# Transposes of q, k and the softmax moved from TensorE to VectorE and DMA, one group's values in one go, the narrow gates in another place

## The chip, the cores and the metric

The kernel runs on one core of a Trainium2 chip. The metric is device time in microseconds (us) of one execution of the whole program; less is better. The engines are named as the profile names them: PE (TensorE: matmuls, and PEld its weight loads), DVE (VectorE), ACT (ScalarE), POOL (GpSimd) and SP (SyncE, which here only issues DMAs).

## What is computed

Two layers of a decoder on 512 tokens of width 1024, all in float32. Each layer has a recurrent branch and an attention branch from one wide projection, gates that merge the two, an output projection, and a gated MLP. The attention has 12 heads of 128 in three groups with dilations 1, 4 and 16, whose results are merged by their softmax sums.

```python
def reference(x, positions, ln1_g, w_in, ...):
    for l in range(DEPTH):
        h = rms_norm(x, ln1_g[l])
        z = h @ w_in[l]                      # 1024 -> 8704 columns
        xr, gr, q, k, v, g_rnn, g_att = jnp.split(z, cuts, axis=-1)
        xr = causal_depthwise_conv(xr, rnn_conv_w[l], rnn_conv_b[l])
        hr = rg_lru(xr, lru_wa[l], ...)       # h_t = a_t h_(t-1) + u_t, both from gates of 128x128 blocks
        y_rnn = hr * jax.nn.gelu(gr)
        y_att = dilated_attention_mixer(q, k, v, positions, q_norm_g[l], k_norm_g[l])
        merged = jax.nn.sigmoid(g_rnn) * (y_rnn @ proj_rnn[l]) + jax.nn.sigmoid(g_att) * (y_att @ proj_attn[l])
        x = x + merged @ w_out[l]
        h2 = rms_norm(x, ln2_g[l])
        u = causal_depthwise_conv(h2 @ w_up[l], ffn_conv_w[l], ffn_conv_b[l])
        u_gate, u_val = jnp.split(u, 2, axis=-1)
        x = x + (jax.nn.gelu(u_gate) * u_val) @ w_down[l]
```

Ahead of the scores, q and k are normalised and rotated per head; the probabilities of a group are weighted by its share of the merged softmax and multiplied with the values.

## The kernel before

**Matmuls.** A float32 product is made of three matmuls on operands split into a high and a low part (`mm3`, L257 to L260: high by high, low by high, high by low). The weights come in 320 units of 512 KB from DRAM into one of two buffers (`wraw<-wst`, issued by SP); ACT casts the unit to its high part (`whi`, L228), DVE subtracts to get the low part (`wlo`, L233), each into one of three buffers. A unit is used by 24 matmuls of 512 columns. The cast of a unit may start when PE has left the unit three before it, so it runs two units ahead of its use.

**Groups.** `layer_groups` lists the groups of 512 output columns of a layer in the order in which PE takes them: N1 P1 v0 va P2 N2 P3 P4 vb (q, k and v of the attention; N for the dilation of 1, P for the two others), then xr0 gr0 xr1 gr1 (recurrence and its GeLU gate), ga0 pa0 ga1 pa1 (gate and projection of the attention), gn0 pr0 gn1 pr1 (gate and projection of the recurrence), wo0 wo1 and the MLP.

**Chains.** What follows a group on ACT and DVE, and the small matmuls of scores, values and recurrent gates, is written as generators (chains) that yield `need(engine, time, ...)`. While the main loop records the large matmuls, a planner with a model of each engine's time records steps of these chains between them, as soon as the model holds their operands for ready and a buffer is free (21 slots of 128x512, 12 quads of 128x2048 and a few PSUM banks). A group that needs the result of chains (pa0, pa1, pr0, pr1) forces the rest of them to be recorded first. The order on each engine is thus fixed when the program is built; at run time the engines only wait for each other's results.

**Transposes.** In `QK.block` (L633) each 128x512 piece of q and k (four heads, or four streams of them) is turned by four PE matmuls against an identity (`transpose`, L263, seen as L264) into a PSUM bank; ACT and DVE split it from there. In `attention` (L751), for each of the four passes of a layer, `values_perm` (L813) and `values_nat` (L844) turn the weighted probabilities in the same way, two banks each; `values_nat`, for the dilation of 1, does turn, split and matmuls for one half and then for the other. Each layer so has 156 such matmuls, 312 in all.

**The recurrence.** `lru_weights` (L876) loads and splits the 128x128 gate blocks; it waits for the chain of the fourth attention pass. `XR` (L899) then makes gates, scan and result, one chain for each half (xr0, xr1), each with three quads and more; `GR` (L963) multiplies the GeLU gate's columns by the scan's result and splits the product into the operands of pr0 and pr1, with two quads, after the XR chain of its half.

## Time and profile before

| | before |
|---|---|
| time, median of 3 runs | 1874.34 us (1870.73 to 1874.37) |
| the profiled execution's own time | 1873.33 us |
| its span, first to last instruction | 1871.5 us |
| PE busy | 1862.1 us, 99% of the span |
| DVE busy | 1243.6 us, 66% |
| ACT busy | 951.6 us, 51% |
| granted TensorE clock, mean | 0.999 of full speed |
| DMA | 194 MB, mean 104 GB/s; queue of the weights 28.3% of 16 engines |

PE's busy time is that of the modelled ends of its matmuls, and neighbours overlap; what one matmul costs is read from the distance between two starts. The page's line for an engine counts busy time and instructions; "idle before" in a group is the engine's idle time just ahead of its instructions, with what ended it.

### The profile page before, as it was taken

The numbers are of one execution on the slowest core, as the hardware profiler recorded it, in microseconds if no ns is written. First come the engines' busy times: TensorE is split into PE (matmuls) and PEld (weight loads), VectorE is DVE, ScalarE is ACT, GpSimd is POOL, SyncE is SP. The second block draws the span as 40 slices with busy tenths as digits, with TensorE's granted clock in tenths as the row PEclk, the third lists the DMA queues.
The fourth block names the chain that finished last, engine by engine and source line by source line (L and its number), as shares of the span: only waits on it lengthen the run. The fifth ranks groups of instructions, "written<-read, shape, count | busy, mean of one in ns | idle before, by whom it ended". The sixth has DMA issues, their size and how long they took to land.

```text
span 1871.5 us, 22327 instructions
## 1 busy us (share of the span) xinstructions
PE 1862.1 (99%) x8561; PEld 1547.1 (83%) x8561; DVE 1243.6 (66%) x1858; ACT 951.6 (51%) x1655; POOL 5.6 (0%) x12
## 2 busy tenths in 40 slices
PE   9999999999999999999999999999999999999999
PEld 7888888888888888888888888888888888888887
DVE  7859976884466763577377599778644677536662
ACT  7758855952344342344365687568423444323441
POOL 0000000000000000000000000000000000000000
PEclk9999999999999999999999999999999999999999
DMA  5232233222322222222332322322223222222222
GB/s 177 96 126 95 85 114 113 79 98 96 144 90 102 90 103 100 90 96 96 127 125 86 130 95 102 104 101 79 102 98 138 91 101 91 101 102 90 102 102 90
DMA packets 68106, 194.07 MB, mean 104 GB/s; under 512 B 17312, under 2 KB 17568, under 8 KB 67488
## 3 DMA queue, kind: packets, MB, share of 16 engines
q1 hardware_dynamic: 61824, 183.97, 28.3%
q0 software_dynamic: 1664, 8.39, 1.3%
q8 instruction: 67, 1.10, 0.2%
q10 hardware_dynamic: 4512, 0.30, 0.2%
q14 instruction: 39, 0.32, 0.1%
HBM read 184.19 MB, written 8.44 MB: 103 GB/s over the span
## 4 chain that ended last, share of the span: by engine, by line
PE 97%; DVE 1%; DMA 1%; ACT 1%; issue 0%; ACTq 0%; DVEq 0%
PE acc L258 31%; PE acc L260 31%; PE acc L259 31%; PE at L264 2%; DVE slot L233 1%; PE at L259 1%; PE at L258 1%; PE at L260 1%; PE y L833 1%; PE at L739 0%; DMA stp<-stats 0%; DMA stats<-st 0%; DMA wraw<-wst 0%; PE y L834 0%; PE y L259 0%; PE y L260 0%
## 5 line engine op out<-in xcount | busy, mean ns | idle before, releaser
L228 ACT CAST whi<-wraw 128x1024 fp32r<-128x1024 f32 (+1 forms) x321 | 334.7, 1043 | 596.4 <-PE acc L259 512.5
L233 DVE TENSOR_TENSOR wlo<-wraw,whi 128x1024 fp32r<-128x1024 f32 (+1 forms) x321 | 390.4, 1216 | 253.4 <-ACT whi L228 253.2
L258 PE MATMUL acc<-xh,whi 128*128 128x512 f32 x1280 | 501.1, 391 | 0.0
L260 PE MATMUL acc<-xh,wlo 128*128 128x512 f32 x1280 | 498.4, 389 | 0.0
L259 PE MATMUL acc<-xl,whi 128*128 128x512 f32 x1280 | 498.2, 389 | 0.0
L260 PEld LDWEIGHTS acc<-xh,wlo 128*128 128x128 f32 x1280 | 240.3, 188 | 50.5
L259 PEld LDWEIGHTS acc<-xl,whi 128*128 128x128 f32 x1280 | 240.5, 188 | 48.7
L258 PEld LDWEIGHTS acc<-xh,whi 128*128 128x128 f32 x1280 | 240.4, 188 | 48.6
L258 PE MATMUL acc<-quad,whi 128*128 128x512 f32 x640 | 249.0, 389 | 0.0
L259 PE MATMUL acc<-quad,whi 128*128 128x512 f32 x640 | 249.0, 389 | 0.0
L260 PE MATMUL acc<-quad,wlo 128*128 128x512 f32 x640 | 249.0, 389 | 0.0
L258 PE MATMUL acc<-whi,xh 128*128 128x512 f32 x576 | 231.4, 402 | 1.7 <-ACT whi L228 1.7
L259 PE MATMUL acc<-wlo,xh 128*128 128x512 f32 x576 | 225.5, 391 | 0.2 <-DVE wlo L233 0.2
L260 PE MATMUL acc<-whi,xl 128*128 128x512 f32 x576 | 225.5, 392 | 0.0
L233 DVE TENSOR_TENSOR slot<-acc,rbc 128x512 f32<-128x512 f32 x120 | 82.7, 689 | 129.4 <-PE acc L260 129.4
L258 PEld LDWEIGHTS acc<-quad,whi 128*128 128x128 f32 x640 | 120.2, 188 | 24.9
L259 PEld LDWEIGHTS acc<-quad,whi 128*128 128x128 f32 x640 | 120.2, 188 | 24.9
L260 PEld LDWEIGHTS acc<-quad,wlo 128*128 128x128 f32 x640 | 120.2, 188 | 24.9
L260 PEld LDWEIGHTS acc<-whi,xl 128*128 128x128 f32 x576 | 108.4, 188 | 23.7
L258 PEld LDWEIGHTS acc<-whi,xh 128*128 128x128 f32 x576 | 108.6, 189 | 22.3 <-ACT whi L228 2.2
L259 PEld LDWEIGHTS acc<-wlo,xh 128*128 128x128 f32 x576 | 108.8, 189 | 21.1 <-DVE wlo L233 1.1
L228 ACT CAST quad<-quad 128x512 fp32r<-128x512 f32 x80 | 49.8, 623 | 82.3 <-DVE quad L233 82.2
(142 smaller groups left out, 1928.2 us busy)
## 6 DMA issues: line engine op xcount, KB each, us to landing
wraw<-wst SPq DMA_DIRECT2D x319, 512.0 KB, 3.2
quad<-xT SPq DMA_DIRECT2D x16, 256.0 KB, 5.4
vorder<-quad POOLq DMA_DIRECT2D x4, 1024.0 KB, 5.6
quad<-vorder POOLq DMA_DIRECT2D x4, 1024.0 KB, 5.8
slot<-gqk SPq DMA_DIRECT2D x12, 256.0 KB, 3.5
slot<-lruw SPq DMA_DIRECT2D x8, 256.0 KB, 5.1
xdram<-quad SPq DMA_DIRECT2D x8, 256.0 KB, 2.9
quad<-xdram SPq DMA_DIRECT2D x8, 256.0 KB, 5.3
```

The costliest lines, as they stand in the source:

```text
L228: nc.scalar.copy(out, src)
L233: nc.vector.tensor_tensor(out, a, b, op=op)
L258: nc.tensor.matmul(ps, rr(ah), rr(bh), start=first, stop=False)
L259: nc.tensor.matmul(ps, rr(ah), rr(bl), start=False, stop=False)
L260: nc.tensor.matmul(ps, rr(al), rr(bh), start=False, stop=last)
L264: nc.tensor.transpose(out, src, ident)
L833: nc.tensor.matmul(yp[:, o:o + 256].rearrange("p (k t) -> p k t", k=2), rr(w[:, 2, b]), rr(w[:, 0:2, b]), start=i == 0, stop=False)
```

## The change

- A new helper `turn` transposes a 128x512 (or 128x384) tile. DVE transposes each of its 32x32 pieces by itself into a slot (one instruction); SP issues four DMAs of 32 partitions each from the slot to a DRAM tile, written in 128-byte pieces so that the 32x32 pieces land exchanged; and, after a planned 3 us, SP issues one DMA from there back into the tile. 
- `QK.block` uses it for every piece of q and k, in place of four PE transposes and a PSUM bank. The splits read the tile from SBUF.
- In `attention`, the weighting of the probabilities is a chain `weigh` for each of four pieces of a pass, and each ends in a `turn`. `values_perm` and `values_nat` then only split and multiply.
- `values_nat` makes both halves' splits first and all its matmuls behind them in one go.
- In `layer_groups` both narrow gates gn0 and gn1 now stand ahead of pr0 and pr1 (before: gn0 pr0 gn1 pr1).

A layer has 40 turns (24 of q and k, 16 of probabilities), the program 80.

```diff
--- before.py
+++ after.py
@@ -75,6 +75,7 @@
         out.append((f"pa{j}", "proj_attn", 4, 0, [(512 * j, 512 * j + 512)]))
     for j in range(2):
         out.append((f"gn{j}", "w_in", 8, 0, [(6656 + 512 * j, 7168 + 512 * j)]))
+    for j in range(2):
         out.append((f"pr{j}", "proj_rnn", 8, 0, [(512 * j, 512 * j + 512)]))
     for j in range(2):
         out.append((f"wo{j}", "w_out", 8, 0, [(512 * j, 512 * j + 512)]))
@@ -371,6 +372,24 @@
 
         def bank_done(t):
             at_free[at_free.index(float("inf"))] = t
+
+        def turn(t, e):
+
+            yield need("dve", e, s=1)
+            n = size(t) // 128
+            slot = salloc()
+            w = slot[:, 0:128 * n]
+            nc.vector.transpose(w, t)
+            e = on_dve(128 * n, e)
+            yield need("pe", e)
+            d = dr.tile([128, 128 * n], F32, name="turn", tag=f"turn{n}", bufs=8)
+            v = d.rearrange("(e c) (j i r) -> c j i e r", e=4, j=n, i=4)
+            for i in range(4):
+                nc.sync.dma_start(v[:, :, i], w[32 * i:32 * i + 32].rearrange("c (j e r) -> c j e r", j=n, e=4))
+            yield need("pe", T["pe"] + 3000.0)
+            free(slot)
+            nc.sync.dma_start(t, d)
+            return T["pe"] + 4000.0
 
         def small(shape, name, bufs=4):
             return sm.tile([128] + shape, F32, name=name, tag=name, bufs=bufs)
@@ -657,12 +676,8 @@
                     w = t.rearrange("p (j k d) -> p j k d", j=2, k=2)
                     rq = rs[:, r].rearrange("p k j -> p j k").unsqueeze(3).to_broadcast([128, 2, 2, 128])
                     e = tt(w, w, rq, ALU.mult, max(e, self.t_rs))
-                yield need("pe", e, at=1)
-                ps = bank()
-                for j in range(4):
-                    transpose(ps[:, j * 128:j * 128 + 128], t[:, j * 128:j * 128 + 128])
-                free(t)
-                t = T["pe"]
+                t3 = yield from turn(t, e)
+                ps, t = t, t3
                 if self.name in IN_ORDER:
                     bl = slice(r * 128, r * 128 + 128)
                     ps = ps.rearrange("p (j t) -> p j t", j=4)
@@ -677,7 +692,7 @@
                     yield need("dve", t)
                     for g in range(2):
                         t = tt(rr(ws[g][:, :, 1]), ps[:, g], ws[g][:, :, 0], ALU.subtract, t)
-                bank_done(t)
+                free(self.qg[r])
 
         class V:
             def __init__(self, l, name):
@@ -786,16 +801,16 @@
             nc.sync.dma_start(d.rearrange("b a r -> (b a) r"), f[:, 0])
             nc.sync.dma_start(f0, d.rearrange("b a r -> (a r) b"))
             t_f0 = t + HOP
-            yield need("act", t)
-            for r in range(4):
-                t = act(p12[:, r], p12[:, r], AF.Copy, t, scale=f[:, 1, r:r + 1])
-            yield need("act", t, s=1, y=2, after=(v_done["v0"], v_done["va" if s < 2 else "vb"]))
+            subs = [start(g, prio) for h in range(2) for g in (
+                weigh(flat[:, 1024 + 512 * h:1536 + 512 * h], [(p12[:, r], f[:, 1, r:r + 1]) for r in (2 * h, 2 * h + 1)], t),
+                weigh(flat[:, 128 + 512 * h:640 + 384 * h], [(p0[:, b], f0[:, b:b + 1]) for b in ((0, 1, 2), (3,))[h]], t_f0))]
+            yield need("act", t, s=1, y=2, after=subs + [v_done["v0"], v_done["va" if s < 2 else "vb"]])
             y_free[0] -= 2
             yp = ps_y.tile([128, 512], F32, name="y", tag="y")
             y0 = ps_y.tile([128, 512], F32, name="y", tag="y")
             va = vt["va" if s < 2 else "vb"]
             y = salloc()
-            subs = [start(values_perm(s, p12, yp, va, t, y), prio), start(values_nat(s, p0, y0, vt["v0"], f0, t_f0), prio)]
+            subs = [start(values_perm(s, flat, yp, va, y), prio), start(values_nat(s, flat, y0, vt["v0"]), prio)]
             yield need("dve", after=subs)
             free(pq)
             t = tt(y, y, y0, ALU.add, max(c.end for c in subs))
@@ -810,7 +825,15 @@
             if s == 3:
                 free(vt["v0"])
 
-        def values_perm(s, p12, yp, va, t_p, y):
+        def weigh(piece, rows, t):
+
+            yield need("act", t)
+            for p, f in rows:
+                t = act(p, p, AF.Copy, t, scale=f)
+            t = yield from turn(piece, t)
+            yield need("act", t)
+
+        def values_perm(s, flat, yp, va, y):
 
             yield need("act", q=1)
             w = qalloc()
@@ -818,12 +841,7 @@
             yv = y.rearrange("p (a r) -> p r a", r=4)
             e = 0.0
             for h in range(2):
-                yield need("pe", t_p, at=1)
-                ps = bank()
-                for i in range(4):
-                    transpose(ps[:, i * 128:i * 128 + 128], p12[:, 2 * h + i // 2, (i % 2) * 128:(i % 2) * 128 + 128])
-                t = yield from split(w[:, 0], w[:, 1], ps, T["pe"])
-                bank_done(t)
+                yield from split(w[:, 0], w[:, 1], flat[:, 1024 + 512 * h:1536 + 512 * h])
                 vh, vl = (w[:, k].rearrange("p (r g d) -> p r g d", r=2, g=2) for k in (2, 3))
                 t = yield from split(vh, vl, vs[:, 2 * h:2 * h + 2, :, s % 2])
                 yield need("pe", max(t, e))
@@ -841,30 +859,27 @@
                 e = tt(yv[:, 2 * h:2 * h + 2], yv[:, 2 * h:2 * h + 2], m[:, :, 1], ALU.add, e)
             free(w)
 
-        def values_nat(s, p0, y0, v0, f0, t_f0):
-            yield need("act", s=4)
-            vh, vl, ph, pl = salloc(), salloc(), salloc(), salloc()
+        def values_nat(s, flat, y0, v0):
+            yield need("act", s=2)
+            vh, vl = salloc(), salloc()
             vh4, vl4 = vh.rearrange("p (r d) -> p r d", r=4), vl.rearrange("p (r d) -> p r d", r=4)
             yield from split(vh4, vl4, v0[:, :, s * 128:s * 128 + 128])
-            yield need("act", t_f0)
-            for b in range(4):
-                t = act(p0[:, b], p0[:, b], AF.Copy, t_f0, scale=f0[:, b:b + 1])
+            parts = []
             for h in range(2):
-                yield need("pe", t, at=1)
-                ps = bank()
                 n = 512 - 128 * h
-                for i, j in enumerate((h, h + 2)):
-                    transpose(ps[:, i * 256:i * 256 + 128], p0[:, j, 128:256])
-                    if j < 3:
-                        transpose(ps[:, i * 256 + 128:i * 256 + 256], p0[:, j + 1, 0:128])
-                t = yield from split(ph[:, 0:n], pl[:, 0:n], ps[:, 0:n], T["pe"])
-                bank_done(t)
-                yield need("pe", t)
-                for i, j in enumerate((h, h + 2)):
-                    m = 256 if j < 3 else 128
-                    b, q = slice(j * 128, j * 128 + 128), slice(i * 256, i * 256 + m)
-                    mm3(y0[:, j * 128:j * 128 + m], vh[:, b], vl[:, b], ph[:, q], pl[:, q], j == 0, j == 3)
-            free(vh, vl, ph, pl)
+                yield need("act", s=2)
+                ph, pl = salloc(), salloc()
+                t = yield from split(ph[:, 0:n], pl[:, 0:n], flat[:, 128 + 512 * h:128 + 512 * h + n])
+                parts.append((ph, pl))
+            yield need("pe", t)
+            for j in (0, 2, 1, 3):
+                ph, pl = parts[j // 2]
+                m = 256 if j < 3 else 128
+                b, o = slice(j * 128, j * 128 + 128), 256 * (j % 2)
+                mm3(y0[:, j * 128:j * 128 + m], vh[:, b], vl[:, b], ph[:, o:o + m], pl[:, o:o + m], j == 0, j == 3)
+            for ph, pl in parts:
+                free(ph, pl)
+            free(vh, vl)
 
         def start_attention(s, *names):
             me = {}
```

What follows is the order of instructions as both kernels are built.

The first place is SP's queue at the start of layer 0, where the blocks of N1 and P1 are turned. `wraw<-wst` is a unit of weights, `turn<-slot` a write to the DRAM tile, `slot<-turn` the read back. Before:

```order
L387 DMA wraw<-wst 128x1024 x7
L766 DMA stp<-stats 128x8
L387 DMA wraw<-wst 128x1024 x2
L786 DMA back<-f 128x4
L787 DMA f_1082<-back 128x4x1
```

Now:

```order
L406 DMA wraw<-wst 128x1024 x2
L388 DMA turn<-slot 128x4x32 x12
L406 DMA wraw<-wst 128x1024
L391 DMA slot<-turn 128x512 x3
L388 DMA turn<-slot 128x4x32 x4
L406 DMA wraw<-wst 128x1024
L391 DMA slot<-turn 128x512
```

Between the loads of the weights there now stand the writes of three turns, their reads, and the next turn; the four writes of a turn wait for its DVE instruction, its read for all four.

The second place is DVE ahead of pr0 in layer 0. `slot<-acc,rbc` empties a PSUM bank of a projection, `quad<-quad` at L920 (now L935) is the scan of the recurrence, and other `quad<-quad` are steps of XR and GR. Before, ahead of and behind the gates of gn0:

```order
L233 TENSOR_TENSOR quad<-quad 128x512 x2
L233 TENSOR_TENSOR wlo_85<-wraw,whi_82 128x1024
L233 TENSOR_TENSOR quad<-quad 128x512
L233 TENSOR_TENSOR wlo_86<-wraw,whi_83 128x1024
L233 TENSOR_TENSOR wlo_87<-wraw,whi_84 128x1024
L233 TENSOR_TENSOR slot<-acc,rbc 128x512 x2
L233 TENSOR_TENSOR wlo_85<-wraw,whi_82 128x1024
```

Now:

```order
L234 TENSOR_TENSOR slot<-acc,rbc 128x512
L234 TENSOR_TENSOR quad<-quad 128x512
L935 SCALAR_TENSOR_TENSOR quad<-quad 128x512
L234 TENSOR_TENSOR slot<-acc,rbc 128x512
L234 TENSOR_TENSOR quad<-quad 128x512
L935 SCALAR_TENSOR_TENSOR quad<-quad 128x512
L234 TENSOR_TENSOR quad<-quad 128x512
L935 SCALAR_TENSOR_TENSOR quad<-quad 128x512
L234 TENSOR_TENSOR quad<-quad 128x512
L935 SCALAR_TENSOR_TENSOR quad<-quad 128x512
L234 TENSOR_TENSOR quad<-quad 128x512 x8
L234 TENSOR_TENSOR wlo_87<-wraw,whi_84 128x1024
```

Before, the steps of GR lie among several units of weights and the gate's banks come after them; now the gate's last banks, the four scans of xr1 and eight steps of GR stand in a row with no unit of weights between them.

The third place is ACT at the same point. `quad<-at,hb` is the first step behind the recurrent gates' matmuls (two banks at once), `quad<-quad` of 2048 columns the square root for all four chunks, `quad<-quad` of 512 columns as CAST the high part of pr0's operand. Now:

```order
L223 ACTIVATE quad<-at,hb 128x512 x2
L223 ACTIVATE quad<-quad,sp_169 128x512 x2
L223 ACTIVATE quad<-quad 128x512
L229 CAST whi_83<-wraw 128x1024
L223 ACT_TABLE_LOAD
L223 ACTIVATE quad<-quad 128x2048
L223 ACT_TABLE_LOAD
L223 ACTIVATE slot<-slot 128x512 x4
L229 CAST whi_84<-wraw 128x1024
L229 CAST quad<-quad 128x512 x4
L229 CAST whi_82<-wraw 128x1024
```

From the last gates of the recurrence to the casts of pr0's operand there are two units of weights left on ACT. On PE, 42 matmuls stand between the last matmul of the recurrent gates and pr0's first in the changed kernel, and 255 in the kernel before.

## Rows read from the trace of the kernel before

**Rows 1.** The page's busy times, and the chain that ended last by line.

```profile
PE 1862.1 (99%) x8561; PEld 1547.1 (83%) x8561; DVE 1243.6 (66%) x1858; ACT 951.6 (51%) x1655; POOL 5.6 (0%) x12
...
PE acc L258 31%; PE acc L260 31%; PE acc L259 31%; PE at L264 2%; DVE slot L233 1%; PE at L259 1%; PE at L258 1%; PE at L260 1%; PE y L833 1%; PE at L739 0%; DMA stp<-stats 0%; DMA stats<-st 0%; DMA wraw<-wst 0%; PE y L834 0%; PE y L259 0%; PE y L260 0%
```

**Rows 2.** Groups by form: busy us, mean ns, idle before, what ended it.

```profile
L233 DVE TENSOR_TENSOR wlo<-wraw,whi 128x1024 fp32r<-128x1024 f32 x319 | 389.0, 1219 | 252.1 <-ACT whi L228 251.9
L228 ACT CAST whi<-wraw 128x1024 fp32r<-128x1024 f32 x319 | 333.4, 1045 | 595.0 <-PE acc L259 512.5 <-PE acc L260 48.8 <-issue 26.4
...
L233 DVE TENSOR_TENSOR slot<-acc,rbc 128x512 f32<-128x512 f32 x120 | 82.7, 689 | 129.4 <-PE acc L260 129.4
...
L264 PE MATMUL at<-const,slot 128*128 128x128 f32 x192 | 28.0, 273 | 2.3 <-DVE dd L233 1.5 <-DVE slot L233 0.9
...
L228 ACT CAST quad<-at 128x512 fp32r<-128x512 f32 x32 | 18.4, 583 | 16.3 <-PE at L264 16.3
L264 PE MATMUL at<-const,quad 128*128 128x128 f32 x120 | 17.9, 273 | 0.0
```

**Rows 3.** PE in order of time: start us, us, instructions.

```profile
81.05 0.39 PE L260 MATMUL acc<-whi,xl 128*128 128x512 f32 x1
81.28 0.60 PE L264 MATMUL at<-const,slot 128*128 128x128 f32 x4
81.64 0.48 PE L258 MATMUL acc<-whi,xh 128*128 128x512 f32 x1
81.95 0.40 PE L259 MATMUL acc<-wlo,xh 128*128 128x512 f32 x1
82.18 0.40 PE L260 MATMUL acc<-whi,xl 128*128 128x512 f32 x1
```

**Rows 4.** PE in order of time: last recurrent gate of layer 0, first matmul of pr0.

```profile
378.79 0.39 PE L260 MATMUL at<-slot,quad 128*128 128x512 f32 x1
...
436.81 0.39 PE L258 MATMUL acc<-quad,whi 128*128 128x512 f32 x1
```

**Rows 5.** ACT in order of time, layer 0's recurrence and GeLU chain.

```profile
375.08 1.24 ACT L222 ACTIVATE quad<-at,hb 128x512 f32<-128x512 f32 x2
376.22 1.67 ACT L222 ACTIVATE quad<-quad,sp 128x512 f32<-128x512 f32 x2
...
390.67 0.63 ACT L222 ACTIVATE quad<-quad 128x512 f32<-128x512 f32 x1
391.32 1.28 ACT L222 ACT_TABLE_LOAD   x1
392.61 1.92 ACT L222 ACTIVATE quad<-quad 128x2048 f32<-128x2048 f32 x1
...
408.31 0.62 ACT L228 CAST quad<-quad 128x512 fp32r<-128x512 f32 x1 [0.93 <-DVE quad L233]
```

**Rows 6.** DVE in order of time, a step of XR and its scan.

```profile
396.64 0.68 DVE L233 TENSOR_TENSOR quad<-quad 128x512 f32<-128x512 f32 x1
397.36 1.22 DVE L920 TENSOR_TENSOR_SCAN quad<-quad 128x512 f32<-128x512 f32 x1
398.50 0.67 DVE L233 TENSOR_TENSOR quad<-quad 128x512 f32<-128x512 f32 x1
```

**Rows 7.** Windows at the start: busy us per engine (count), clock, DMA share, GB/s.

```profile
8.00:9.00 1.00, 1.00 (x3) 0.50 (x2) 0.36 (x1) 0.67 (x1) 0.00 (x0) 0.50 1.03 379
11.00:12.00 1.00, 1.00 (x6) 0.78 (x5) 1.00 (x3) 1.00 (x3) 0.00 (x0) 1.00 1.03 334
```

**Rows 8.** DMA issues: queue, count, KB each, median us to landing.

```profile
slot<-gqk SPq DMA_DIRECT2D x12, 256.0 KB, 3.5
...
xdram<-quad SPq DMA_DIRECT2D x8, 256.0 KB, 2.9
...
stats<-st ACTq DMA_DIRECT2D x8, 4.0 KB, 4.5
```

**Rows 9.** Windows around one stats<-st write, columns as in rows 7.

```profile
92.50:93.00 0.50, 0.50 (x5) 0.46 (x4) 0.08 (x1) 0.50 (x2) 0.00 (x0) 1.00 0.10 2
93.00:93.50 0.50, 0.50 (x4) 0.41 (x3) 0.47 (x2) 0.41 (x2) 0.00 (x0) 1.00 0.40 7
```

**Rows 10.** Windows by stage in layer 0: attention, recurrence.

```profile
55.00:318.00 263.00, 262.14 (x1338) 221.39 (x1337) 202.02 (x377) 179.10 (x442) 2.74 (x4) 1.00 0.31 103
318.00:420.00 102.00, 102.00 (x451) 84.49 (x451) 90.12 (x121) 77.37 (x101) 0.00 (x0) 1.00 0.25 87
```

## Prediction

> **What bounds the kernel now.** I read the busy times first, then the chain that ended last [rows 1]. PE is busy in 1862.1 of 1871.5 us, so all waits of PE in the whole program come to 9.4 us. The chain says the same from the other side: nearly all of its lines are large matmuls, and the transposes (at L264) are on it with 2%. The kernel is bound by the number of PE instructions at the full clock, and there are two ways to change its time: fewer or cheaper instructions on PE, or a new wait of PE. Then I read the groups [rows 2] for what one operation costs, and PE in order of time for what a transpose costs PE, which is not its duration. Last come the places that the new order makes tight: PE's arrival at pr0, and the chain of ACT and DVE that it then needs [rows 4 to 6].
>
> **Transposes off PE.** A row of four transposes begins at 81.28 and the next matmul at 81.64; that matmul's successor comes 0.31 later, where matmuls otherwise come every 0.227 us (81.05 to 81.28) [rows 3]. So four cost 0.36 + (0.31 - 0.227) = 0.44 us. There are 192 + 120 of them [rows 2], 78 groups of four: 78 x 0.44 = **-34.3 us**. The chain's 2% (28 to 47 us by its rounding) holds that number. Where they stand PE has no other work to hide in, so it is a gain in full, as long as nothing waits instead.
>
> **What turns cost on DVE and ACT.** No row shows the 32x32 transpose. The nearest below is a tensor operation of the same shape, 0.69 us [rows 2], the nearest above the scan, 1.22 us [rows 6]; I take 0.69, since one operand is read and one written as in most rows of that shape. 40 a layer are 28 us. In the attention's stretch DVE is busy 202 of 263 us [rows 10], so it rises to 87%; in the recurrence's stretch it is busy 90 of 102 us already and PE loses nothing there [rows 10]. I cost it at nothing; at 1.22 it is a rival below. ACT keeps its casts; from PSUM a 128x512 cast took 0.58 us, from SBUF 0.62 [rows 2, 5].
>
> **What turns cost in time.** A PE transpose lies 0.36 us ahead of the cast. A turn takes 0.69 on DVE, then a write and a read. The nearest rows for a write are xdram (256 KB in large pieces, 2.9 us) and stats (512 pieces of 8 bytes, 4.5 us), for the read slot<-gqk, 3.5 us [rows 8]: 7.1 to 8.7 us together. What the order leaves for it: of the 80 turns 71 stand three or more units of weights ahead of the cast that reads them (three units are 3 x 24 x 0.227 = 16.3 us), and 9 only two units (10.9 us). On SP a read waits for its writes, and what stands behind it waits too; if that adds one write, 2.9 us, the slow path is 11.6 us, 0.7 late for each of the nine: **+6 us**. The bounds are 0 (the fast path everywhere) and 9 x (8.7 + 4.5 - 10.9) = 21 us. The loads of weights behind a waiting read have slack: a cast starts when PE leaves its buffer, two units ahead (casts wait for PE in 561 of the 595 us of idle time before them [rows 2]), so after cast and subtraction 10.9 - 1.05 - 1.22 = 8.6 us are left.
>
> **DMA itself.** The stats write kept the 16 engines 0.10 + 0.40 of half-microseconds busy [rows 9], 0.25 us for 512 pieces. A write of a turn has 512 pieces too, four writes make 1 us; with 256 KB each way at the pace of 379 GB/s [rows 7] a turn takes some 2.4 us of the engines, 40 turns 96 us. The share in the attention's stretch rises from 0.31 to about 0.67 [rows 10]. That is no bound by itself.
>
> **Values in one go.** The matmuls of `values_nat` are the same; their operands must all be there first. Nothing in the order puts a group behind it, so I cost it at nothing. What it may cost is inside the bounds of the turns.
>
> **The gates moved, and a new wait ahead of pr0.** This is the term on which the sign rests. The recurrent gates start only when the fourth attention pass has ended, and turns make each pass longer, so the order has XR and GR later among the groups. Before, 57.8 us lie between the last recurrent gate (379.01) and pr0 (436.81) [rows 4]. Gate gn1 ahead of pr0 gives 4 units, 21.8 us, but now 42 matmuls are all that stands between: 42 x 0.227 = 9.5 us. What must happen in that time, from the end of the last gate at 0: on ACT a pair of 1.24, a pair of 1.67, a square of 0.63 [rows 5]; the cast of a unit of weights whose buffer PE frees after 18 matmuls, at 4.1, until 5.15; a table load of 1.28 and the square root of 1.92, which begin as they do at 391.32 and 392.61 [rows 5], until 8.4. On DVE the gate's banks and a wlo stand in between, so xr1's first product starts at about 9.35. Four products and scans, 1.86 each by their starts (396.64 to 398.50) [rows 6], with one bank of 0.6 between them: 17.4. The two quads of GR's first chain are free only now, so its product (0.76 with the hop) and cast (0.62) end at 18.85. PE waits 9.3 us. Then it has the high part only; the low part and the second chunk cost two more waits, together 1.8: 11.1 us. In the third unit of pr0 the operand comes from GR's second half, whose casts stand on ACT behind that of a unit whose buffer PE frees late: 1.95 of products, 0.5, 0.8 and 0.5, another 3.75. Per layer 14.9, and the order is the same in both layers: **+29.7 us**. The bounds are 0 (the chain is early, because PE waits further ahead in any case) and 36: a second table load and root (1.28 + 1.92) on the chain in each layer.
>
> **The clock.** At the start, after PE has been idle, three matmuls begin in a microsecond at a granted clock of 0.50 (1.2 GHz), and six at 1.00 (2.4 GHz) [rows 7]. A wait of 9 us may bring that again. If it holds 3 us as at the start, half of them are lost: 1.5 a layer, **+3 us**.
>
> **Sum.** 1873.3 (the profiled execution's own time, 1.0 below the median) - 34.3 + 29.7 + 3 + 6 = 1877.7, and with that 1.0 **1879 us**. By the bounds it would be 1840 to 1900.
>
> **The rivals.**
> *A. The wait ahead of pr0 does not come.* PE waits a little at many turns, and ACT and DVE run ahead of the order there. For it speaks that casts wait for PE in most of their idle time [rows 2], so both engines catch up fast; against it, that the chain counted above starts with a PE instruction and cannot begin earlier. 1873.3 - 34.3 + 6 + 1 = **1846**, faster.
> *B. Small writes hold SP's queue.* Each read waits on SP until all four writes of 128-byte pieces have landed, and loads of weights stand behind it. Where six turns stand within three units (the densest place), three reads in a row that wait 4.5 us for their writes [rows 8] make 13.5 us, 4.9 more than the 8.6 of slack above. With five such places in the two layers +25 us beside the other terms: **1904**, slower. It decides from about 2.9 us of landing on. For it speaks the 4.5 us of stats, against it the share of 0.31 [rows 10].
> The 8-byte pieces of stats land in 4.5 us although they are 4 KB, and xdram's 256 KB in 2.9 [rows 8]. The Trainium skill ("DMA: Bandwidth & Descriptors", Specifications) says that line rate wants at least 512 bytes and that less is read, modified and written; by that rule the 128-byte pieces are slow ones, which is this rival. The trace agrees for 8 bytes and has no row for 128.
> *C. DVE's transposes cost as much as a scan.* At 1.22 us [rows 6], 202 + 40 x 1.22 = 251 of 263 us [rows 10]. Six turns within three units are 7.3 us where DVE has 23% of 16.3 = 3.8 free, so 3.5 late; three such bunches a layer, 21 us: **1900**, slower.
>
> **How the numbers follow.** A measurement of this kernel can tell about 0.2%, 3.7 us: the same is 1870.6 to 1878.1. The forecast has 0.60; its own range is 1862 to 1896, and of it 0.10 lies faster, 0.25 the same and 0.25 slower, since its two largest terms nearly cancel. A has 0.16, B 0.14, C 0.10. Faster 0.10 + 0.16 = 0.26, same 0.25, slower 0.25 + 0.14 + 0.10 = 0.49. The range runs from 1850 to 1908: it leaves out more than half of A, a third of B and the tails of the others, 0.19 in all.
>
> **What would show it.** In the changed kernel's profile: the groups of transposes at L264 are gone and PE's busy time is about 34 lower. PE idles some 9 us ahead of the first acc<-quad of pr0 in each layer, ended by ACT's cast of a quad or DVE's product, and again in its third unit; a granted clock near 0.5 follows. DVE's transpose has a mean near 0.69. turn<-slot lands in 2.9 to 4.5 us and waits of PE in the attention are short and many. The forecast is wrong if PE goes into pr0 without a wait (A), if PE waits for wlo or whi and these for wraw, with SP waiting for a turn (B), or if DVE is late with its own work in the attention (C).

## The result and the profile after

The changed kernel takes 1956.2 us (median of 4 runs, 1954.35 to 1957.61) against 1874.33: a ratio of 1.0441, 95% interval 1.0423 to 1.0459. It is 82 us slower, 77 more than forecast and outside the range. Its profiled execution took 1954.35 us.

The page of the changed kernel: busy times, the granted clock in 40 slices, the chain by line.

```profile
PE 1868.8 (96%) x8249; PEld 1535.6 (79%) x8249; DVE 1306.6 (67%) x1938; ACT 967.2 (50%) x1655; POOL 5.6 (0%) x12
...
PEclk9999998999899999999999998989999999999999
...
PE acc L259 22%; PE acc L260 22%; PE acc L261 22%; DVE slot L234 5%; DMA slot<-turn 3%; SPq L388 3%; DVE wlo L234 3%; DVE quad L234 2%; DMA turn<-slot 2%; ACT junk L223 1%; ACT whi L229 1%; ACT quad L229 1%; ACT quad L223 1%; DMA stats<-st 1%; DVE slot L382 1%
```

PE has 312 instructions less, as it should, and idles 1952.6 - 1868.8 = 83.8 us where it idled 9.4 [rows 1]. The large matmuls held 31% of the chain for each of their lines and hold 22% now; DVE, ACT, SP's queue and the turn's DMAs have come onto it. The clock, 0.999 before, has slices at 0.8. Four windows hold nearly all of it (columns as in [rows 7]): the attention and the start of pr0, in each layer. The last line is a part of the first wait ahead of pr0.

```profile
55.00:350.00 295.00, 266.35 (x1197) 218.60 (x1196) 224.27 (x398) 176.33 (x421) 2.75 (x4) 0.95 0.58 154
...
475.00:515.00 40.00, 28.51 (x108) 20.94 (x107) 25.47 (x34) 18.30 (x23) 0.00 (x0) 0.87 0.15 53
...
1030.00:1345.00 315.00, 290.07 (x1294) 238.04 (x1293) 228.55 (x406) 188.35 (x423) 2.61 (x4) 0.95 0.58 158
...
1445.00:1485.00 40.00, 28.51 (x106) 20.90 (x105) 25.05 (x34) 17.00 (x21) 0.00 (x0) 0.87 0.15 53
...
489.00:493.00 4.00, 0.00 (x0) 0.00 (x0) 3.62 (x4) 0.29 (x1) 0.00 (x0) 0.50 0.00 0
```

Attention: PE is idle 28.6 + 24.9 = 53.6 us. Start of pr0: it is idle 11.5 us in each layer. What the clock costs can't be read from a window's mean: the last line shows 0.50 while PE is still waiting, and a slow clock costs nothing there. I took the distances between the starts of PE's matmuls instead, against the median for the same shapes in the kernel before. What a matmul that had to wait comes late is a wait, and what a distance at 0.50 is longer is the clock. In the attention of both layers that gives 59.4 us of waits and 24.9 of slow clock, at the start of pr0 25.8 and 5.9. In the whole program both together are 113.4 us more than before, and the rest of PE's work is 32.4 us less: +81, as measured between the two profiled executions. So the place that the forecast priced at +33 costs 32, and the place that it priced at +6 costs 84.

**The wait ahead of pr0** runs as it was counted. PE of the changed kernel in layer 0, and below it ACT and DVE there:

```profile
474.46 0.39 PE L261 MATMUL at<-slot,quad 128*128 128x512 f32 x1
...
483.98 0.39 PE L261 MATMUL acc<-xh,wlo 128*128 128x512 f32 x1
493.38 0.80 PE L259 MATMUL acc<-quad,whi 128*128 128x512 f32 x1 [9.01 <-ACT quad L229]
...
509.14 0.50 PE L259 MATMUL acc<-quad,whi 128*128 128x512 f32 x1 [1.47 <-ACT quad L229]
```

```profile
474.26 1.32 ACT L223 ACTIVATE quad<-at,hb 128x512 f32<-128x512 f32 x2
...
481.10 1.92 ACT L223 ACTIVATE quad<-quad 128x2048 f32<-128x2048 f32 x1
...
492.71 0.62 ACT L229 CAST quad<-quad 128x512 fp32r<-128x512 f32 x1 [4.56 <-DVE quad L234]
```

```profile
484.03 0.68 DVE L234 TENSOR_TENSOR quad<-quad 128x512 f32<-128x512 f32 x1
...
490.87 1.22 DVE L935 TENSOR_TENSOR_SCAN quad<-quad 128x512 f32<-128x512 f32 x1
```

The last recurrent gate ends at 474.7 (its start and 0.227). From there the root ends at 483.0 (8.3; forecast 8.4), the first product starts at 484.0 (9.3; 9.35), the cast ends at 493.3 (18.6; 18.85) and PE has waited 9.01 us (9.3). The wait in pr0's third unit is shorter than forecast, 1.47 us for 3.75.

**A turn** in the attention is another matter. SP of the changed kernel in layer 0 (start, us, DMA issues; a merged row spans all its issues), then the DVE, ACT and PE rows that belong to the first three turns:

```profile
52.02 9.35 SPq L406 DMA_DIRECT2D wraw<-wst  x2
61.41 8.18 SPq L388 DMA_DIRECT2D turn<-slot  x12
69.69 0.56 SPq L406 DMA_DIRECT2D wraw<-wst  x1
70.30 1.42 SPq L391 DMA_DIRECT2D slot<-turn  x3
```

```profile
55.13 1.89 DVE L382 STREAM_TRANSPOSE slot<-slot 128x512 f32<-128x512 f32 x3
```

```profile
74.74 1.93 ACT L229 CAST quad<-slot 128x512 fp32r<-128x512 f32 x3 [7.89 <-DMA slot<-turn]
...
77.91 1.25 ACT L223 ACTIVATE quad<-acc,rc 128x512 f32<-128x512 f32 x2
```

```profile
78.64 0.50 PE L259 MATMUL acc<-whi,xh 128*128 128x512 f32 x1 [3.42 <-ACT quad L223]
```

DVE has turned the three tiles by 57.0. SP stands until 61.4 at a load of weights whose buffer is not free. Then the twelve writes take 8.2 us to issue, another load passes, and the reads go out at 70.3. ACT has waited 7.9 us by the time that it casts at 74.7, and everything behind that cast in its order is late. So is the emptying of two PSUM banks (`quad<-acc,rc`, 77.91), and PE's first wait in the attention, until 78.64, is for such a bank. Waits of PE for ACT's L223 are the longest group outside pr0:

```profile
PE acc L259 <- ACT quad L223: 16.8, 7, 4.3
```

The instructions of line and tile `turn` in all (min/median/max ns on the issuing engine), and who waited for them:

```profile
L388 SPq DMA_DIRECT2D turn<-slot x320: 569/627/2752, 61.4 to 1336.4; - x160
...
  ACT quad L229: 127.9, 30
  ACT slot L229: 8.2, 3
```

I paired the 80 turns of the trace by their tiles. The mean way from the end of the DVE instruction to the landing of the read is 16.0 us: 5.0 until the first write is issued, 2.8 for issuing four, 2.2 until the last has landed, 1.9 until the read is issued, 4.1 for the read (these are the means of the 80, from the starts and landings of the DMAs).

### The profile page after: what moved, and what is told of

It reads as the page before. It is cut to its first block, busy times and chain, and to the rows that moved or that the text cites. A ratio compares the mean times of both kernels' runs of the same rounds, so it can differ in the third digit from the quotient of the medians.

```text
span 1952.6 us, 22350 instructions
## 1 busy us (share of the span) xinstructions
PE 1868.8 (96%) x8249; PEld 1535.6 (79%) x8249; DVE 1306.6 (67%) x1938; ACT 967.2 (50%) x1655; POOL 5.6 (0%) x12
## 4 chain that ended last, share of the span: by engine, by line
PE 69%; DVE 12%; DMA 8%; ACT 5%; SPq 4%; issue 2%; ACTq 0%; DVEq 0%
PE acc L259 22%; PE acc L260 22%; PE acc L261 22%; DVE slot L234 5%; DMA slot<-turn 3%; SPq L388 3%; DVE wlo L234 3%; DVE quad L234 2%; DMA turn<-slot 2%; ACT junk L223 1%; ACT whi L229 1%; ACT quad L229 1%; ACT quad L223 1%; DMA stats<-st 1%; DVE slot L382 1%
## 5 line engine op out<-in xcount | busy, mean ns | idle before, releaser
L259 PE MATMUL acc<-xh,whi 128*128 128x512 f32 x1280 | 506.0, 395 | 13.7 <-ACT quad L223 10.8
L260 PE MATMUL acc<-xl,whi 128*128 128x512 f32 x1280 | 503.3, 393 | 0.0
L259 PEld LDWEIGHTS acc<-xh,whi 128*128 128x128 f32 x1280 | 243.6, 190 | 65.8 <-ACT quad L223 12.9
L259 PE MATMUL acc<-quad,whi 128*128 128x512 f32 x640 | 252.0, 394 | 22.1 <-ACT quad L229 22.0
L260 PE MATMUL acc<-quad,whi 128*128 128x512 f32 x640 | 251.8, 393 | 0.9 <-DVE quad L234 0.9
L234 DVE TENSOR_TENSOR slot<-acc,rbc 128x512 f32<-128x512 f32 x112 | 77.1, 689 | 109.9 <-PE acc L261 109.9
L261 PEld LDWEIGHTS acc<-quad,wlo 128*128 128x128 f32 x640 | 121.2, 189 | 24.9
L229 ACT CAST quad<-slot 128x256 fp32r<-128x256 f32 (+1 forms) x104 | 62.3, 638 | 138.9 <-DMA slot<-turn 127.9
```

The costliest lines, as they stand in the source:

```text
L229: nc.scalar.copy(out, src)
L234: nc.vector.tensor_tensor(out, a, b, op=op)
L259: nc.tensor.matmul(ps, rr(ah), rr(bh), start=first, stop=False)
L260: nc.tensor.matmul(ps, rr(ah), rr(bl), start=False, stop=False)
L261: nc.tensor.matmul(ps, rr(al), rr(bh), start=False, stop=last)
```

## The experiments

**Theories.** One: the loss in the attention is SP's queue (issue time of 320 writes, writes behind loads that wait). Two: the casts stand too close behind their turn in the order, so that ACT, which works in order, waits and holds up what stands behind them. Rival B of the prediction: loads of weights come late behind the writes. Times of before in these comparisons are 1872.7 to 1873.6 us.

**Only the gates moved**, without turns:

```diff
     for j in range(2):
         out.append((f"gn{j}", "w_in", ...))
+    for j in range(2):
         out.append((f"pr{j}", "proj_rnn", ...))
```

> The kernel before with only the narrow gates moved (gn0 gn1 pr0 pr1), no turns. Both theories (the loss in the attention comes from SP's queue of turns, or from casts that the order puts too close behind their turn) give 1870 to 1879 us: without turns the recurrence ends in time and the 57.8 us between the last recurrent gate and pr0 stay. The rival that the moved gates alone make the wait ahead of pr0 gives about 1874 + 2 x (11.5 + 5 of slow clock) = 1907 us.

1873.19 us, ratio 1.0002 (0.9992 to 1.0011). The move alone does nothing that can be measured, and makes no wait ahead of pr0.

**All turns, gates in the old order** (the edit above taken out of the changed kernel):

> The changed kernel with the gates in the old order (gn0 pr0 gn1 pr1). If the wait ahead of pr0 comes from the late recurrence, as I forecast, then taking four units (21.8 us) from between makes it longer: 1956 + up to 2 x 21.8, 1975 to 2000 us, with PE idle 20 to 31 us ahead of pr0. If the moved gates made it, the wait is gone: 1956 - 33 = 1923 us.

2006.5 us, ratio 1.0705 (1.0681 to 1.0729), a little above the forecast. PE there in layer 0:

```profile
478.95 0.80 PE L258 MATMUL at<-slot,quad 128*128 128x512 f32 x1 [6.45 <-ACT slot L228]
496.98 0.79 PE L258 MATMUL acc<-quad,whi 128*128 128x512 f32 x1 [14.81 <-ACT quad L228]
```

The wait ahead of pr0 grows to 14.8, and the recurrent gates now wait too. So the late recurrence makes this wait, and the gates' move saves 50 us there: from the recurrent gates to pr0, waits and slow clock come to 83 us in the two layers of this run, to 32 in the changed kernel (by the distances between starts).

**Turns on POOL:**

```diff
-                nc.sync.dma_start(v[:, :, i], w[...])
+                nc.gpsimd.dma_start(v[:, :, i], w[...])
...
-            nc.sync.dma_start(t, d)
+            nc.gpsimd.dma_start(t, d)
```

> The changed kernel with the five DMAs of a turn issued by POOL instead of SP, nothing else. Theory one, SP's queue (320 writes at 0.63 us of issue each, and writes standing behind loads of weights that wait for their buffer): PE's waits outside pr0 (58 us) and the slow clock there (31 us) mostly go, 1880 to 1905 us, and ACT waits for slot<-turn and quad<-turn far less than 136 us. Theory two, the order leaves too little time behind a turn whatever queue it takes: 1945 to 1960 us.

1920.8 us, ratio 1.0259 (1.0242 to 1.0276): 35 us back of 82, less than theory one wanted and more than theory two. The order of instructions on ACT and DVE is the same in both traces. A turn takes 13.7 us instead of 16.0 (3.1 instead of 5.0 to the first write), and ACT's waits fall, as the tile's row of this run shows:

```profile
  ACT quad L229: 82.3, 24
...
  ACT slot L229: 10.6, 2
```

**The read 9 us behind the writes:**

```diff
-            yield need("pe", T["pe"] + 3000.0)
+            yield need("pe", T["pe"] + 9000.0)
```

> The changed kernel with the planner told that the read back may be issued 9 us after the writes instead of 3, so casts are recorded later. Theory two (distance in the order): PE's waits in the attention fall by half or more, 1905 to 1930 us, less what the later recurrence costs ahead of pr0. Theory one (SP's issue time): the reads move, the issue time stays, 1940 to 1970 us.

1950.6 us, ratio 1.0414 (1.0398 to 1.0429). I took that for theory one, wrongly: the paired turns show that the edit held the read back as well (7.8 us from landing to read instead of 1.9, 22.8 for the whole way), and ACT still waits 105.5 us for turned tiles. A run below changes the cast alone.

**Writes alone, nobody waiting:**

```diff
+        def price(n):
+            d = dr.tile([128, 128 * n], F32, name="turn", ...)
+            for i in range(4):
+                nc.sync.dma_start(v[:, :, i], const[32 * i:32 * i + 32, ...])
```

> The kernel before, its PE transposes kept, with four writes of 128-byte pieces to a DRAM tile added on SP at each of the 80 places where the changed kernel has a turn; they read a constant, nobody reads them back. It prices SP's issue time and DMA load when nobody waits for the result. If the loss of the changed kernel comes from weights that are late behind the writes (my rival B), this loses 20 us and more: 1895 to 1935. If it comes from the turn's own way to ACT's cast, and weights have their slack, 1874 to 1882 us.

1880.5 us, ratio 1.0038 (1.0023 to 1.0053). The same 320 writes with their issue time (median 0.627 us), in the kernel before, cost 7.5 us (4 to 10 by the interval). PE's waits for whi or wlo are 1.3 us in all. So the writes alone don't make the loss. The reads, which rival B has waiting on SP ahead of the loads, are not in this run; the trace of the changed kernel has them:

```profile
SPq L391 <- DMA turn<-slot: 19.2, 33, 2.1
```

```profile
ACT whi L229 <- DMA wraw<-wst: 20.6, 12, 3.6
```

No read waits there for its writes for more than 2.1 us, where rival B needed 4.5. ACT waits for late weights 20.6 us (6.7 in the kernel before), against 136 for turned tiles, and PE 4.8 us for wlo. So in the changed kernel rival B is at most a small part of the loss.

**Writes recorded at once:**

```diff
             e = on_dve(128 * n, e)
-            yield need("pe", e)
```

> The changed kernel with the writes of a turn recorded right behind its DVE transpose, so that on SP they stand ahead of the next load of weights instead of behind it (in the changed kernel three transposes end at 57.0 and their writes begin at 61.4, behind a load that waits for its buffer). If standing behind loads is the larger part of a turn's way, the waits in the attention fall by half: 1905 to 1930 us. If the 0.63 us of each issue is, 1940 to 1955 us. Ahead of pr0 54 matmuls stand instead of 42: 2.7 us less of wait in each layer.

1972.7 us, ratio 1.0535 (1.0517 to 1.0553), slower, which neither theory had. A turn takes 13.4 us, as on POOL; but with its writes the planner put read and cast earlier too, so that ACT still waits for turned tiles (119.9 and 12.3 us). It is not the way alone that counts, but the way against the place of the cast. Why the run is 16 us slower than the changed kernel was not taken apart.

**Softmax alone, on SP**, and **q and k alone, on POOL** (the other part written as before):

> The changed kernel with q and k turned by PE as before; only the probabilities go by DVE and DMA (32 turns, on SP), gates moved. 294 matmuls (66 us) stand between the last recurrent gate and pr0, so the wait there, 33 us with its slow clock, goes. PE's gain is 30 groups by 0.44 = 13 us. By theory one (SP) the 32 turns cost what they cost in the changed kernel in the waits of values (y matmuls), 10 to 20 us: 1870 to 1885 us.

1899.9 us, ratio 1.0146 (1.0131 to 1.0161). The wait ahead of pr0 is gone, but a new one has come:

```profile
PE acc L259 <- DVE quad L234: 16.3, 2, 8.2
```

This is pa0 waiting for PSUM banks that DVE empties behind four scans of the recurrence, once in each layer; ACT waited 21 us for turned probabilities.

> q and k turned by DVE and DMA, issued by POOL; the probabilities turned by PE as before, gates moved. 171 matmuls (39 us) stand ahead of pr0, so no wait there. PE's gain is 48 groups by 0.44 = 21 us. Waits of PE for ACT behind late q and k as with both on POOL, some 13 us, with 10 us of slow clock: 1870 to 1885 us; below 1868 it beats the kernel before.

1893.5 us, ratio 1.0113 (1.0095 to 1.0131). No wait ahead of pr0, but 18.7 us of waits of the score matmuls for DVE, and ACT waits 79.5 us for turned tiles. Each half alone, with the casts where the planner's 4 us put them, loses more than its transposes are worth.

**Casts 12 us behind the read, all else as in the changed kernel:**

```diff
-            return T["pe"] + 4000.0
+            return T["pe"] + 12000.0
```

> The changed kernel, all DMAs on SP and recorded as there; only the planner's figure for when the turned tile may be read goes from 4 to 12 us behind the read's issue, so casts are recorded later. In the changed kernel a turn takes 16 us from the end of its DVE instruction to its landing. If the loss in the attention is ACT's casts standing too early in its order, PE's waits there (58 us and 31 us of slow clock) fall by half: 1905 to 1930 us, with the wait ahead of pr0 unchanged (it has 42 matmuls ahead of it as before). If the loss is the longer chain itself, the waits move to where its end is needed and the time stays: 1945 to 1970 us.

1911.7 us, ratio 1.0206 (1.0189 to 1.0223). One number of the planner gives back 44.5 of the 82 us, on the same queue and with turns that take 17.6 us, longer than before. Who waits for the turns, and PE's longest waits:

```profile
  DVE quad L234: 12.1, 1
  ACT quad L229: 1.8, 2
```

```profile
PE acc L259 <- ACT quad L229: 22.0, 6, 9.0
PE y L851 <- DVE quad L234: 15.0, 3, 10.9
PE acc L259 <- DVE quad L234: 6.3, 2, 6.0
```

ACT's 136 us of waits are gone, as theory two has it. The 22.0 are pr0's, as before; the others are values and large matmuls behind DVE. But SP's queue shows in another place: ACT now waits for late weights. The sum of these waits, then SP, ACT and PE around PE's longest wait:

```profile
ACT whi L229 <- DMA wraw<-wst: 112.1, 33, 13.1
```

```profile
1171.86 7.59 SPq L388 DMA_DIRECT2D turn<-slot  x8
...
1180.20 3.41 SPq L388 DMA_DIRECT2D turn<-slot  x4
1183.71 2.27 SPq L406 DMA_DIRECT2D wraw<-wst  x1
```

```profile
1189.42 1.04 ACT L229 CAST whi<-wraw 128x1024 fp32r<-128x1024 f32 x1 [13.09 <-DMA wraw<-wst]
...
1196.93 0.55 PE L851 MATMUL y<-quad 128*128 128x256 f32 x1 [10.86 <-DVE quad L234]
```

The load stands behind the writes of three turns. ACT waits 13.1 us for those weights and DVE 12.1 for a turned tile, and the values wait behind both.

**With 15 us:**

> All turns on SP, casts planned 15 us behind the read instead of the 12 of the run that took 1911.7. If waits for turned tiles remain there, 1895 to 1908; if not, 1908 to 1920, since what is left is pr0 and waits of the values for DVE.

1914.7 us, ratio 1.0223 (1.0208 to 1.0238): no waits of ACT for turns remain, and the time stays. More distance doesn't help: pr0's 22.0 us are left, and ACT's waits for weights on SP, 118.3 us.

**Both remedies, the read recorded right behind its writes on POOL:**

```diff
-            yield need("pe", T["pe"] + 3000.0)
-            free(slot)
-            nc.sync.dma_start(t, d)
-            return T["pe"] + 4000.0
+            nc.gpsimd.dma_start(t, d)
+            yield need("pe", T["pe"] + 6000.0)
+            free(slot)
+            return T["pe"] + 6000.0
```

> Both remedies at once: turns on POOL, the read issued as soon as its writes have landed, casts planned 12 us behind it. If queue and order are the whole loss of the attention, what is left is -34 for the transposes and +33 ahead of pr0: 1873 to 1890 us. If the longer chain costs by itself, 1905 to 1925.

2004.5 us, ratio 1.0712 (1.0687 to 1.0736), the opposite of what I expected. POOL in layer 0 shows why, first here and then with the read held back as in the changed kernel (4 to 12 us, on POOL):

```profile
55.90 3.07 POOL L388 DMA_DIRECT2D turn<-slot  x4 [55.45 <-DVE slot L382]
61.05 0.56 POOL L389 DMA_DIRECT2D slot<-turn  x1 [2.09 <-ACT slot L223]
61.61 2.94 POOL L388 DMA_DIRECT2D turn<-slot  x4
66.99 0.56 POOL L389 DMA_DIRECT2D slot<-turn  x1 [2.43 <-ACT sd L223]
```

```profile
57.07 8.97 POOL L388 DMA_DIRECT2D turn<-slot  x12 [56.62 <-DVE slot L382]
66.03 0.57 POOL L391 DMA_DIRECT2D slot<-turn  x1
```

> All turns on POOL, casts planned 12 us behind the read as in the 1911.7 us run, and the read recorded 3 us behind the writes as in the changed kernel, so that it does not hold up the next turn's writes as it did in the 2004 us run. If that order of reads made the 2004, this gives 1895 to 1915 us; if POOL with late casts is slow in itself, 1950 and more.

1896.1 us, ratio 1.012 (1.0105 to 1.0135). With each read directly behind its writes, POOL waits for their landing before it issues the next turn's writes, 5.7 us for each turn, and the mean way is 19.7 us. Held back, three turns' writes go out in a row; way 14.9 us. (The cast is planned 15 us behind the writes here, and 12 in the 2004 us run; on SP, 3 us more changed nothing.)

This run completes a square: 1956.2 on SP and 1920.8 on POOL with casts at 4 us, 1911.7 and 1896.1 with casts at 12. ACT and DVE have the same order on both queues. So the queue is worth 35 us with early casts and 16 with late ones, where ACT's waits for weights go from 112.1 to 15.8 us, and the place of the casts is worth 44 us on SP and 25 on POOL. Both theories hold in part.

**q and k of some groups alone**, with that same serial order on POOL:

> Only q and k of N1, P1, N2 and P3 are turned, on POOL and planned as in the run before; P2, P4 and the probabilities stay on PE; gates moved. 285 and 351 matmuls stand ahead of pr0, so no wait there. 32 groups by 0.44 us are 14 us of gain; if late casts are all that costs, 1860 to 1870 us, else 1872 to 1885.

> As the run before with N2 and P3 alone, 16 groups: a gain of 7 us if nothing waits, 1866 to 1869 us; 1871 to 1880 if the longer way to the scores costs.

1892.6 (ratio 1.0107, 1.0092 to 1.0122) and 1899.4 us (1.0143, 1.0128 to 1.0158). Turns take 17.7 and 16.9 us there, more than the 12 the planner had, so these two show the serial queue once more and say little about the groups.

**q and k alone, on SP, casts 12 us behind the read:**

> q and k alone turned, DMAs on SP, casts planned 12 us behind the read; the probabilities on PE, gates moved. 138 matmuls (31 us) stand ahead of pr0, so no wait there: if casts that stand too early and pr0 are the whole loss, -21 for 48 groups and a few us of waits: 1856 to 1866 us, faster than before. If a longer way from q and k to the scores costs by itself, 1872 to 1890.

1857.1 us, ratio 0.9912 (0.9898 to 0.9927): faster than both kernels. **With 15 us:**

> As the run before with 15 us instead of 12: fewer late casts, the recurrence a little later (138 and 102 matmuls ahead of pr0). If late casts are what remains, 2 to 6 us faster than the run before; if the length of the chain is, equal or slower.

1863.8 us, ratio 0.9954 (0.9938 to 0.9971); the longer chain costs 7 us and the later casts save nothing. Then the 12 us with the **DMAs on POOL**, and with **writes on POOL, reads on SP**:

> The 1857 us kernel (q and k alone, casts planned 12 us behind the read) with the turns' DMAs on POOL. Where all turns are made, POOL for SP gave 1896 for 1912. If SP's queue still costs when casts stand late enough, 1850 to 1855 us; if its waits are covered now, 1855 to 1860 us.

> As the run before with the writes on POOL and the reads on SP, so that neither queue holds the other's next step: 1850 to 1857 us if the queues still matter, 1857 as on SP alone if not; slower than 1860 if SP's reads, which wait for POOL's writes, hold up the weights.

1851.1 us, ratio 0.9877 (0.9861 to 0.9894), and 1850.1 us, ratio 0.9874 (0.9859 to 0.9889). The two don't differ by their intervals; for q and k alone SP's queue costs some 6 us when the casts stand late enough (16 with all turns). The place of the casts alone is worth 42 us here: with 4 us and all else equal, the same turns on POOL took 1893.5. Page and waits of PE with all DMAs on POOL:

```profile
PE 1841.4 (100%) x8369; PEld 1527.8 (83%) x8369; DVE 1285.8 (70%) x1906; ACT 972.9 (53%) x1657; POOL 173.5 (9%) x252
```

```profile
PE at L754 <- DVE quad L238: 1.2, 1, 1.2
PE at L458 <- DVE bias L469: 1.2, 1, 1.2
PE acc L259 <- ACT whi L229: 1.1, 2, 0.9
```

All of PE's waits are a few us, and 48 groups of transposes give 22.4 us, 0.47 each.

## Why the prediction was wrong, point by point

**Transposes off PE: right.** 0.44 us a group was forecast; the 22.4 us of 48 groups, with hardly a wait left, are 0.47. In the changed kernel PE's own work fell by 32.4 us where 34.3 were forecast.

**DVE: right.** The 32x32 transpose of a 128x512 tile takes 0.70 us, and rival C is out:

```profile
L382 DVE STREAM_TRANSPOSE slot<-slot 128x512 f32<-128x512 f32 x48 | 33.1, 701 | 0.7
```

**What turns cost in time: the step that failed.** It gave 7.1 to 8.7 us for a turn, +6 us for the kernel and 21 as the upper bound; it measured 16.0 us for a turn and some 84 us, idle time and slow clock together. Four pieces were wrong. The issue of the three writes ahead of the last was not counted at all (2.1 of the 2.8 us). The first write stands 5.0 us and the read 1.9 us behind other entries of SP, of which the forecast had one write of 2.9 on the slow path only. And the distance of three units, 16.3 us, which it took for ample, is the mean way itself, so it was not 9 of 80 turns that came late: ACT waited for turned tiles 33 times. The error was to set a turn's duration against a distance, when its place in a queue decides when it begins. The square of runs shows both parts of it, the queue and the place of the casts. [rows 8] show landings alone. How long the issuing engine is held stands in the trace of before too, 0.37 us for one `stats<-st` on ACT's queue, but was not looked up.

**The waits' consequence was mis-sized too.** A late cast was priced by its own lateness. On ACT it holds up what stands behind it, the emptying of PSUM banks above all (16.8 us of PE's waits), and PE then pays again with a slow clock: the clock's term was 3 us, and it is 5.9 us at pr0 and 24.9 in the attention.

**The wait ahead of pr0: right.** 14.9 us of wait and 1.5 of clock a layer were forecast, 12.9 and 3.0 measured; 32.7 against 31.7 in all. That the totals lie so close is in part luck, since the third unit's wait was forecast too long and the clock too short. Rival A is out. The gates' move alone is neutral, and without it the changed kernel would take 50 us more.

**Rival B** named the right queue and, for the changed kernel, the wrong victim: reads and loads on SP. The writes of 128-byte pieces were not slow to land, 2.2 us behind the last issue, no read waited more than 2.1 us for them, and PE waited 4.8 us for wlo. With late casts on SP the weights do come late to ACT (112.1 us), but behind the writes' issue. How far the rule of the Trainium skill on which the rival leaned ("DMA: Bandwidth & Descriptors", Specifications: line rate wants at least 512 bytes) holds for these writes, no run here takes apart. One of 64 KB landed 3.0 us after its issue at the median, where 256 KB in large pieces took 2.9 [rows 8]. The engines' share in layer 0's attention went from 0.31 at 103 GB/s [rows 10] to 0.58 at 154, more for each byte moved. The estimate for that share, 0.67, was near.

**What stays open.** With all turns, a good queue and late casts, 1896 us remain, 45 more than with q and k alone, although 30 more groups of transposes, some 13 us, are off PE. Of these 58 us the wait ahead of pr0 with its clock is 32. Nearly all of the rest lies in the attention, where waits and slow clock still come to 28 us (84 in the changed kernel). How much of that is the longer chain of the softmax and how much the planner's order around it was not taken apart. Nor was the softmax alone run with late casts.

## What to carry to other kernels

When work moves from an engine to a chain of DMAs, price the whole way: where its first DMA stands in the issuing queue, how long that engine is held for each issue, landing, and where the read stands. Then tell the order (planner, table or hand) that number: here one constant, 12 us for 4, was worth 25 to 44 us. A loss of 4.4% became a gain of 0.9% with that constant and q and k alone, and of 1.2 to 1.3% with their writes on POOL too. On a queue that waits in order, a read right behind its own writes serialises what could overlap.

## What the runs showed of the hardware

A DMA of 512 pieces of 128 bytes held SP for 0.63 us at the median and POOL for 0.74, where the load of 512 KB of weights held SP for 0.33. And the clock fell after a wait of 3.4 us: PE waited until 78.64, and this window of the changed kernel stands at 0.50, the 1.2 GHz level.

```profile
80.00:82.00 2.00, 2.00 (x6) 1.52 (x6) 0.88 (x2) 1.52 (x3) 0.00 (x0) 0.50 0.68 242
```

In the 9-us wait ahead of pr0 the clock fell while PE was still idle (0.50 from 489 to 493), and it stayed there until about 498, 5 us after PE had started again; the start of the run had suggested 3 [rows 7].
